# Conditioning matmuls of the second layer: from the first MLP to the stretches between projections, loaded through ScalarE's DMA queue

## The chip, the cores and the metric

The kernel runs on one core of a Trainium2 chip. TensorE (PE in the profile) multiplies; PEld is its loading of weights. VectorE (DVE) and ScalarE (ACT) do the elementwise work, GpSimd (POOL) masks and a few loads, SyncE (SP) issues most loads. The metric is the device time of one execution in microseconds, lower is better.

## What is computed

A decoder step of two layers over 512 prompt tokens and 32 sample tokens (8 sequences of 4), 544 columns in all, in float32. Every sub-layer is wrapped in two RMS norms, and shift, scale and gate come from a conditioning vector per sequence:

```python
def ada_params(c, w, b):
    mod = jax.nn.silu(c) @ w + b
    return jnp.split(mod[:, None, :], 6, axis=-1)
...
for layer in range(DEPTH):
    sh_m, sc_m, g_m, sh_f, sc_f, g_f = ada_params(c, ada_w[layer], ada_b[layer])
    hin = rmsnorm(x, norm_g[layer, 0]) * (1.0 + sc_m) + sh_m
    ...                                   # layer 0: RG-LRU mixer, layer 1: chunked spatial gate
    x = x + g_m * rmsnorm(mix, norm_g[layer, 1])
    hf = rmsnorm(x, norm_g[layer, 2]) * (1.0 + sc_f) + sh_f
    f = jnp.square(jax.nn.relu(hf @ mlp_w_up[layer])) @ mlp_w_down[layer]
    x = x + g_f * rmsnorm(f, norm_g[layer, 3])
```

The weights ada_w of a layer are 1024 x 6144, 25 MB; there are nine conditioning vectors. The six sections of 1024 columns are called sections 0 to 5 below.

## The kernel before

**Projections.** The activations lie transposed: features on partitions, 544 columns in two halves of 272. A large product is split in three (high x high, high x low, low x high), each a matmul of 128 x 128 weights over 272 columns; all go through the helper `mm` (line 119). Weights come through SyncE's queue into wpool (16 buffers), are split by ScalarE (hi, line 181) and VectorE (lo, line 182) ahead of use.

**Clock and tasks.** `mm` also advances a clock by one tick. Side work is written as generators that are added to this clock: each runs a piece, then yields the number of ticks after which its next piece is due. The code's order sets the priority of instructions; the framework that builds the program orders each engine's instructions by that and by when it expects them to be ready, and puts in the waits. Buffers of a pool (gpool has 26, wpool 16, aux two of PSUM, acc three) are given out as they come free.

**Between two projections.** The last projection of a sub-layer (`final_proj`) computes half 0 of all eight row tiles and then half 1 (144 matmuls). For each half a `Chain` follows as a task: root mean square of the result (`Stat`, whose matmul over partitions is line 390), its reciprocal root (lines 412 to 415), the gated residual (lines 660, 662), a second norm, and then, two row tiles at a time, the scaled (line 448) and shifted input HH and HL (lines 452, 453) of the next projection. The next projection begins with `first_sweeps` (288 matmuls): for each half, over four row tiles of weights and then two, first all products with HH, row tile by row tile as the chain brings them, then those with HL. This happens at three places: from the RG-LRU to the first MLP (`final_proj` with (l, idx) = (0, 1)), from the first MLP to the spatial gate (0, 3), and from the spatial gate to the second MLP (1, 1).

**Conditioning.** `ada_gen(jobs, every)` computes blocks of 2048 columns. Per row tile k (eight to a block) it loads 128 x 2048 weights as two tiles of wpool through SyncE's queue (line 598), one step ahead, and issues four matmuls of 128 x 32 by 128 x 512 into four column groups of one aux buffer (line 609). At the end of a block the sums are copied by ScalarE (line 616), transposed (line 620), added with the bias into MOD (`ada_add`, line 568) and derived (`ada_derive`). For layer 1 three such blocks run in the first MLP, a step every 85 ticks, beside `state_out`, which transposes the recurrent states (line 1237) and stores them:

```python
    chains = mlp(0, (1, 0), chains, [ada_gen([(1, 0), (1, 1), (1, 2)], 85), state_out()])
```

`mlp` adds these tasks after its `first_sweeps`.

Of the kernel before, what the change touches and what calls it, by code (L numbers as in the profile page):

```python
# [12 lines left out]
ALU = mybir.AluOpType  # L13
PSUM = bass.MemoryType.PSUM

P = 128
D = 1024
KD = D // P
# [62 lines left out]
def trunk_kernel(  # L81
# [6 lines left out]
    nc = tc.nc  # L88
    V = nc.vector
    A = nc.scalar  # L90
# [13 lines left out]
    def slot(name, dt=F32):  # L104
        return gpool.tile([P, SLOT], dt, tag="s", name=nm(name))
# [4 lines left out]
    def aux():  # L110
        return auxp.tile([P, 512], F32, tag="aux", name=nm("aux"))
# [4 lines left out]
    clk = Clock()  # L116
# [449 lines left out]
    def ada_add(l, sec, kk, nq, src):  # L566
        b = G1[:, kk:kk + nq, 8 + 6 * l + sec:9 + 6 * l + sec]
        V.tensor_tensor(MOD[l][:, sec, kk:kk + nq, :], src, b.to_broadcast([P, nq, 9]), op=ALU.add)

    def ada_derive(l, idx, k0=0, k1=KD):  # L570
        g = G1[:, k0:k1, 4 * l + idx:4 * l + idx + 1].to_broadcast([P, k1 - k0, 9])
        am = AM[l][idx][:, k0:k1]
        V.scalar_tensor_tensor(am, am, 1.0 if idx % 2 == 0 else 0.0, g, op0=ALU.add, op1=ALU.mult)
        V.tensor_scalar(am, am, -0.5, None, op0=ALU.mult)
# [18 lines left out]
    def ada_gen(jobs, every):  # L593
# [10 lines left out]
        for i, (l, blk, k) in enumerate(steps):  # L604
# [21 lines left out]
                ada_derive(l, idx)  # L626
            yield every - 12

    class Chain:


# [55 lines left out]
    def first_sweeps(key, chains, evac):  # L687

        for h in range(2):
            for grp in ((0, 1, 2, 3), (4, 5)):  # L690
                lhs = [st.get(key(m // 2)).lhs(m % 2) for m in grp]
                ps = [acc() for _ in range(len(grp) // 2)]
                for k in range(KD):
                    chains[h].need(k)
                    for i in range(len(grp)):
                        for a in (0, 1):
                            mm(ps[i // 2][:, i % 2, 0:HW], lhs[i][k][a], HH[:, k, HS[h]], k + a == 0, False)
                for i, m in enumerate(grp):
                    for k in range(KD):
                        mm(ps[i // 2][:, i % 2, 0:HW], lhs[i][k][0], HL[:, k, HS[h]], False, k == KD - 1)  # L700
                    if i % 2:
                        for j in range(2):
                            evac(m - 1 + j, ps[i // 2][:, j, 0:HW], h)

    def mix_add(m, ps, first):
# [3 lines left out]
        else:  # L709
            V.tensor_tensor(mv, mv, ps[:, :, 0:HW], op=ALU.add)  # L710

    def final_proj(lhs, rhs, both, groups, l, idx, nxt):


        A.activation(warm, epsc, AF.Abs_reciprocal_sqrt)
        S = [Stat(), Stat(nxt is None)]
        rows = LastRows(AM[l][idx]) if nxt is None else None
        for m in both:
            ps = acc()
            mm3(ps, lhs(m), rhs, (0, 1))  # L720
            mix_add(m, ps, False)
            for h in range(2):
                S[h].add(MIX[:, m, HS[h]])
        if rows:
            rows.add(both)
        chains = []
        for h in range(2):
            for grp, parts in groups[h]:
                if rows and h == 1 and grp[-1] == KD - 1:
                    rows.residual()  # L730
                if rows and h == 1 and grp[-1] == KD - 1:
                    for j, m in enumerate(grp):
                        ps = acc()
                        mm3(ps, lhs(m), rhs, (1,), col=0)
                        V.tensor_tensor(MIX[:, m, HS[1]], MIX[:, m, HS[1]], ps[:, 0, 0:HW], op=ALU.add)
                        S[1].add(MIX[:, m, HS[1]])
                        rows.finish_tile(j)
                    break
                ps = [acc() for _ in range(len(grp) // 2)]
                for ks in parts:  # L740
                    for i, m in enumerate(grp):
                        mm3(ps[i // 2], lhs(m), rhs, (h,), ks=ks, col=i % 2)
                        if i % 2 and ks is parts[-1]:
                            mv = MIX[:, m - 1:m + 1, HS[h]]
                            V.tensor_tensor(mv, mv, ps[i // 2][:, :, 0:HW], op=ALU.add)
                            S[h].add2(mv, slot("sq")[:, 0:T].rearrange("p (j n) -> p j n", j=2))
                            if rows and h == 1:
                                rows.add((m - 1, m))
            if rows and h == 1:
                rows.finish(S[1])  # L750
            else:
                chains.append(Chain(l, idx, S[h], h, nxt))
        return chains
# [497 lines left out]
    def mlp(l, nxt, chains, tasks):  # L1251
        for q in range(4):
            hh, hl = [None] * 8, [None] * 8

            def evac(m, ps, h=None):
                if hh[m] is None:
                    hl[m] = slot("hl", F32R)
                    hh[m] = slot("hh", F32R)
                w = slot("hf")
                if h is None:  # L1260
                    dl, dh, dw = [t_[:, 0:T].rearrange("p (h n) -> p h n", h=2) for t_ in (hl[m], hh[m], w)]
                else:
                    dl, dh, dw = hl[m][:, HS[h]], hh[m][:, HS[h]], w[:, HS[h]]
                A.activation(dw, ps, AF.Relu)  # L1264
                A.activation(dw, dw, AF.Square)
                A.copy(dh, dw)  # L1266
                V.tensor_tensor(dl, dw, f32(dh), op=ALU.subtract)  # L1267

            if q == 0:
                first_sweeps(lambda c: ("u", l, 0, c), chains, evac)  # L1270
                for t in tasks:
                    clk.add(t)
            for c in range(3 if q == 0 else 0, 4):
                u = st.get(("u", l, q, c))
                for j in range(2):
                    ps = acc()
                    mm3(ps, u.lhs(j), hin_rhs, (0, 1))
                    evac(2 * c + j, ps[:, :, 0:HW])
            rhs = list(zip(hh, hl))
            if q == 3:  # L1280
                return final_proj(lambda m: st.get(("d", l, 3, m // 2)).lhs(m % 2), rhs, (0, 1),
                                  (singles(range(2, 8), 8),) * 2, l, 3, nxt)
            for c in range(4):
                u = st.get(("d", l, q, c))
                for j in range(2):
                    ps = acc()
                    mm3(ps, u.lhs(j), rhs, (0, 1))
                    mix_add(2 * c + j, ps, q == 0)
# [79 lines left out]
    def spatial_gate(chains):  # L1368
# [40 lines left out]
            V.bn_stats(stat[0:NSMP, 4, c, :], v)  # L1409

        first_sweeps(lambda c: ("su", c), chains, u_evac)
        t_prep = clk.add(sg_prepare(), 10)
        vts = []
        for c in range(6):
# [139 lines left out]
                nc.sync.dma_start(y_prompt[0, c0:c1, b * 512:(b + 1) * 512], o[0:n, 0:512])  # L1554
                yield 6

    chains = mlp(0, (1, 0), chains, [ada_gen([(1, 0), (1, 1), (1, 2)], 85), state_out()])
    chains = spatial_gate(chains)
    chains = mlp(1, None, chains, [])
    clk.drain(*[t for t in clk.tasks])  # L1560
# [30 lines left out]
```

## Time and profile before

| | |
|---|---|
| median of 3 runs | 1434.71 us (1432.13 to 1434.84) |
| the profiled execution | 1435.27 us, span 1433.5 us |
| TensorE busy | 1395.7 us, 97% of the span |
| VectorE, ScalarE busy | 703.7 us (49%), 632.5 us (44%) |
| moved | 165.71 MB, mean 116 GB/s |

The profile is of one execution. Times in rows are microseconds from the span's start unless they say ns. Busy TensorE is not TensorE at its best, since matmuls overlap and their ends are modelled; the time of a stretch is better read from its length and its count of matmuls. A float32 matmul stands in the rows as two (x8 for four). A row of windows gives the stretch, its length, then busy time (and count of instructions) of PE, PEld, DVE, ACT and POOL, or of those of them that are asked for, then the granted clock of TensorE as a share of 2.4 GHz, the share of the DMA engines and GB/s. An idle time in brackets is that of the engine just before the instruction, with what ended it.

### The profile page before, as it was taken

How to read it: one execution, taken by the hardware profiler on the slowest of the kernel's cores; microseconds unless marked ns; L12 is line 12 of the kernel's file. 1: busy time of each engine (PE TensorE's matmuls, PEld its weight loads, DVE VectorE, ACT ScalarE, POOL GpSimd, SP SyncE). 2: the span in 40 equal slices, each digit the busy share in tenths (PEclk: the TensorE clock that was granted, in tenths of full speed). 3: DMA queues.
4: the chain of work that ended last, by engine and by line, in shares of the span. 5: the costliest groups of instructions: out<-in, count | busy, mean ns of one | idle time of the engine just before them, and what ended most of it. 6: DMA issues, size and time to landing. Idle time of an engine off the chain costs nothing.

```text
span 1433.5 us, 27033 instructions
## 1 busy us (share of the span) xinstructions
PE 1395.7 (97%) x11472; PEld 1319.4 (92%) x11472; DVE 703.7 (49%) x1442; ACT 632.5 (44%) x1160; POOL 41.1 (3%) x76
## 2 busy tenths in 40 slices
PE   8999999998999999999998999999899999999997
PEld 6899989997999999999997989999899999999996
DVE  4767476779422332333349446653972233333334
ACT  4465746846523413414425434432573341432523
POOL 1200000000100000000000200000000000000000
PEclk8999999999999999999999999999999999999998
DMA  9554554321545545543221333122232222222201
GB/s 309 174 173 130 163 151 149 103 89 60 180 154 174 170 157 173 170 157 115 62 86 60 95 96 107 61 74 62 90 100 91 89 89 89 89 89 89 89 1 63
DMA packets 132227, 165.71 MB, mean 116 GB/s; under 512 B 10168, under 2 KB 111560, under 8 KB 132106
## 3 DMA queue, kind: packets, MB, share of 16 engines
q1 hardware_dynamic: 130346, 161.89, 35.9%
q0 software_dynamic: 1760, 2.09, 0.7%
q8 instruction: 90, 1.47, 0.4%
q14 instruction: 31, 0.25, 0.1%
HBM read 161.31 MB, written 2.65 MB: 114 GB/s over the span
## 4 chain that ended last, share of the span: by engine, by line
PE 65%; issue 26%; DVE 5%; ACT 2%; DMA 1%; POOL 0%; SPq 0%; POOLq 0%; ACTq 0%; DVEq 0%
PE acc L119 58%; PE aux L609 3%; DVE lo L182 1%; PE acc L1478 1%; DVE MIX L448 1%; DVE X L662 1%; DMA xsr<-in_x_sample_dram 1%; DVE HL L453 1%; PE aux L1397 0%; PE aux L580 0%; DVE MIX L660 0%; PE aux L390 0%; ACT HH L452 0%; DVE rs L414 0%; DVE R L415 0%
## 5 line engine op out<-in xcount | busy, mean ns | idle before, releaser
L119 PE MATMUL acc<-HH,hi 128*128 128x272 f32 x1776 | 399.2, 293 | 12.6 <-ACT HH L452 11.2
L119 PE MATMUL acc<-HH,lo 128*128 128x272 f32 x1776 | 394.0, 292 | 3.4 <-DVE lo L182 3.4
L182 DVE TENSOR_TENSOR lo<-raw,hi 128x512 fp32r<-128x512 f32 (+1 forms) x404 | 263.2, 682 | 254.3 <-ACT hi L181 188.1
L119 PE MATMUL acc<-HL,hi 128*128 128x272 f32 x1776 | 355.4, 289 | 3.5 <-DVE HL L453 3.1
L181 ACT CAST hi<-raw 128x512 fp32r<-128x512 f32 (+1 forms) x404 | 230.3, 613 | 281.7 <-PE acc L119 159.2
L119 PEld LDWEIGHTS acc<-HH,hi 128*128 128x128 f32 x1776 | 293.6, 191 | 23.2 <-ACT HH L452 13.7
L119 PEld LDWEIGHTS acc<-HH,lo 128*128 128x128 f32 x1776 | 293.1, 191 | 11.5 <-issue 6.7
L119 PEld LDWEIGHTS acc<-HL,hi 128*128 128x128 f32 x1776 | 273.5, 189 | 10.9 <-issue 5.4
L119 PE MATMUL acc<-hh,lo 128*128 128x272 f32 x1024 | 230.0, 290 | 0.0
L119 PE MATMUL acc<-hh,hi 128*128 128x272 f32 x1024 | 229.8, 290 | 0.0
L119 PE MATMUL acc<-hl,hi 128*128 128x272 f32 x1024 | 229.7, 290 | 0.0
L119 PEld LDWEIGHTS acc<-hh,hi 128*128 128x128 f32 x1024 | 168.0, 188 | 3.9 <-issue 3.8
L119 PEld LDWEIGHTS acc<-hh,lo 128*128 128x128 f32 x1024 | 168.1, 188 | 3.7 <-issue 3.6
L119 PEld LDWEIGHTS acc<-hl,hi 128*128 128x128 f32 x1024 | 168.1, 188 | 3.6 <-issue 3.5
L1267 DVE TENSOR_TENSOR hl<-hf,hh 128x544 fp32r<-128x544 f32 (+1 forms) x76 | 47.7, 634 | 175.2 <-ACT hh L1266 175.0
L1264 ACT ACTIVATE hf<-acc 128x544 f32<-128x544 f32 (+1 forms) x76 | 41.2, 550 | 128.1 <-PE acc L119 126.1
L710 DVE TENSOR_TENSOR MIX<-MIX,acc 128x544 f32<-128x544 f32 x44 | 31.6, 717 | 75.9 <-PE acc L119 75.9
L119 PE MATMUL acc<-hi,HH 128*128 128x256 f32 x192 | 54.8, 285 | 0.0
L119 PE MATMUL acc<-hi,HL 128*128 128x256 f32 x192 | 54.6, 284 | 0.0
L119 PE MATMUL acc<-lo,HH 128*128 128x256 f32 x192 | 53.8, 280 | 0.0
L119 PE MATMUL acc<-yh,hi 128*128 128x272 f32 x208 | 52.7, 291 | 0.3 <-ACT MIX L708 0.3
L119 PE MATMUL acc<-yh,lo 128*128 128x272 f32 x208 | 52.6, 291 | 0.0
(332 smaller groups left out, 1444.5 us busy)
## 6 DMA issues: line engine op xcount, KB each, us to landing
ada<-in_ada_w_dram SPq DMA_DIRECT2D x96, 512.0 KB, 4.9
raw<-in_mlp_w_up_dram SPq DMA_DIRECT2D x64, 512.0 KB, 4.3
raw<-in_mlp_w_down_dram SPq DMA_DIRECT2D x64, 512.0 KB, 4.5
raw<-in_lru_w_in_dram SPq DMA_DIRECT2D x24, 512.0 KB, 4.5
raw<-in_sg_w_in_dram SPq DMA_DIRECT2D x24, 512.0 KB, 4.6
raw<-in_sg_w_out_dram SPq DMA_DIRECT2D x12, 512.0 KB, 4.2
raw<-in_lru_w_out_dram SPq DMA_DIRECT2D x8, 384.0 KB, 3.0
raw<-in_lru_w_out_dram SPq DMA_DIRECT2D x6, 512.0 KB, 6.4
```

The lines of the kernel that those rows point to most:

```text
L119: nc.tensor.matmul(out, lhsT, rhs, start=start, stop=stop)
L181: A.copy(h_, raw[:, c:c + st])
L182: V.tensor_tensor(l_, raw[:, c:c + st], f32(h_), op=ALU.subtract)
L448: V.scalar_tensor_tensor(wv, X[:, k, c0:c1], Am[:, k, 0:1], R[:, c0:c1], op0=ALU.mult, op1=ALU.mult)
L453: V.scalar_tensor_tensor(HL[:, k, c0:c1], wv, sh[:, k, 0:1], f32(HH[:, k, c0:c1]), op0=ALU.add, op1=ALU.subtract)
L609: nc.tensor.matmul(ps[32 * g:32 * g + 32, :], scT[:, k, :], ts_[g // 2][:, (g % 2) * 512:(g % 2) * 512 + 512], start=(k == 0), stop=(k == ...
L662: V.scalar_tensor_tensor(X[:, j, c0:c1], MIX[:, j, c0:c1], Gm[:, j, 0:1], X[:, j, c0:c1], op0=ALU.mult, op1=ALU.add)
L710: V.tensor_tensor(mv, mv, ps[:, :, 0:HW], op=ALU.add)
L1264: A.activation(dw, ps, AF.Relu)
L1267: V.tensor_tensor(dl, dw, f32(dh), op=ALU.subtract)
L1478: nc.tensor.matmul(ps[p0:p0 + 32, 0, ck * P:(ck + 1) * P], vp[ck // 2, c][:, o:o + 32], wT[g], start=True, stop=True, tile_position=(0, p0))
```

## The change

A new generator `ada_fill(l, c0, n)` computes n columns of a layer's conditioning from column c0. It takes a step of four matmuls of the same shape as ada_gen's, of which four times 256 KB of weights are loaded into four slots of gpool ("adf") through ScalarE's DMA queue, one step ahead; 52 ticks lie between steps. With n = 2048 the four column groups of the aux buffer are four blocks of 512 columns, eight steps in all; with n = 1024 they are two blocks of columns for two row tiles at once, four steps, and two of the groups are added by VectorE at the end. The buffer is held from the first step to the last.

Three fills for layer 1 start with the second half of a final projection: sections 0 and 1 at (0, 1), sections 2 and 3 at (0, 3), section 5 at (1, 1). Each is drained behind the first_sweeps that follow. Section 4 is a task of the first MLP, in the place of the three blocks of ada_gen. Layer 0's conditioning stays as it was.

```diff
--- before.py
+++ after.py
@@ -625,6 +625,41 @@
             for idx in ((0,), (1,), (2, 3))[blk]:
                 ada_derive(l, idx)
             yield every - 12
+
+    def ada_fill(l, c0, n, wait=52):
+
+
+        kk = 4096 // n // 2
+        nb = n // 512
+        for k0 in range(0, KD, kk):
+            ts_ = [slot("adf") for _ in range(4)]
+            for g in range(4):
+                k, c = k0 + g // nb, c0 + (g % nb) * 512
+                nc.scalar.dma_start(ts_[g][:, 0:512], ada_w[l, k * P:(k + 1) * P, c:c + 512])
+            yield wait
+            if k0 == 0:
+                ps = aux()
+            for g in range(4):
+                nc.tensor.matmul(ps[32 * g:32 * g + 32, :], scT[:, k0 + g // nb, :], ts_[g][:, 0:512],
+                                 start=(k0 == 0), stop=(k0 + kk == KD), tile_position=(0, 32 * g))
+        raw = slot("adas")
+        A.copy(raw[:, 0:512], ps)
+        yield 12
+        pt = aux()
+        for q in range(4):
+            nc.tensor.transpose(pt[:, q * P:(q + 1) * P], raw[:, q * P:(q + 1) * P], ident)
+        ptv = pt.rearrange("p (q g s) -> p q g s", q=4, g=4)
+        for g in range(4):
+            c = c0 + (g % nb) * 512
+            sec, kt = c // D, (c % D) // P
+            if g < nb:
+                ada_add(l, sec, kt, 4, ptv[:, :, g, 0:9])
+            else:
+                m_ = MOD[l][:, sec, kt:kt + 4, :]
+                V.tensor_tensor(m_, m_, ptv[:, :, g, 0:9], op=ALU.add)
+        for sec in range(c0 // D, (c0 + n) // D):
+            if sec in (1, 2, 4, 5):
+                ada_derive(l, (1, 2, 4, 5).index(sec))
 
     class Chain:
 
@@ -709,6 +744,9 @@
         else:
             V.tensor_tensor(mv, mv, ps[:, :, 0:HW], op=ALU.add)
 
+    fills = {}
+    FILL = {(0, 1): (1, 0, 2048), (0, 3): (1, 2048, 2048), (1, 1): (1, 5 * D, 1024)}
+
     def final_proj(lhs, rhs, both, groups, l, idx, nxt):
 
 
@@ -725,6 +763,8 @@
             rows.add(both)
         chains = []
         for h in range(2):
+            if h == 1 and (l, idx) in FILL:
+                fills[l, idx] = clk.add(ada_fill(*FILL[l, idx]))
             for grp, parts in groups[h]:
                 if rows and h == 1 and grp[-1] == KD - 1:
                     rows.residual()
@@ -1268,6 +1308,7 @@
 
             if q == 0:
                 first_sweeps(lambda c: ("u", l, 0, c), chains, evac)
+                clk.drain(fills[l, 1])
                 for t in tasks:
                     clk.add(t)
             for c in range(3 if q == 0 else 0, 4):
@@ -1409,6 +1450,7 @@
             V.bn_stats(stat[0:NSMP, 4, c, :], v)
 
         first_sweeps(lambda c: ("su", c), chains, u_evac)
+        clk.drain(fills[0, 3])
         t_prep = clk.add(sg_prepare(), 10)
         vts = []
         for c in range(6):
@@ -1554,7 +1596,7 @@
                 nc.sync.dma_start(y_prompt[0, c0:c1, b * 512:(b + 1) * 512], o[0:n, 0:512])
                 yield 6
 
-    chains = mlp(0, (1, 0), chains, [ada_gen([(1, 0), (1, 1), (1, 2)], 85), state_out()])
+    chains = mlp(0, (1, 0), chains, [ada_fill(1, 4 * D, 1024), state_out()])
     chains = spatial_gate(chains)
     chains = mlp(1, None, chains, [])
     clk.drain(*[t for t in clk.tasks])
```

## Rows read from the trace of the kernel before

**Rows 1.** page, busy time of each engine; the chain that ended last, by engine
```profile
PE 1395.7 (97%) x11472; PEld 1319.4 (92%) x11472; DVE 703.7 (49%) x1442; ACT 632.5 (44%) x1160; POOL 41.1 (3%) x76
...
PE 65%; issue 26%; DVE 5%; ACT 2%; DMA 1%; POOL 0%; SPq 0%; POOLq 0%; ACTq 0%; DVEq 0%
```

**Rows 2.** windows, line 119 alone, over equal parts of the two MLPs
```profile
378.91:711.82 332.91, 309.36 (x2403) 302.72 (x2401) 1.00 0.47 151
1068.13:1369.38 301.25, 301.25 (x2403) 301.25 (x2402) 1.00 0.28 86
```

**Rows 3.** the same window of the first MLP, lines 609, 620, 1237
```profile
378.91:711.82 332.91, 25.58 (x192) 3.79 (x192) 1.00 0.47 151
...
378.91:711.82 332.91, 1.80 (x12) 1.42 (x12) 1.00 0.47 151
...
378.91:711.82 332.91, 2.39 (x16) 1.62 (x16) 1.00 0.47 151
```

**Rows 4.** chain of waits, two pieces: start us, us, what
```profile
397.48 0.99 PE aux L609 x8
398.47 10.96 PE acc L119 x85
```

**Rows 5.** windows, all engines, the three stretches between projections
```profile
324.00:358.00 34.00, 27.40 (x187) 25.82 (x186) 32.21 (x76) 20.23 (x46) 0.00 (x0) 0.90 0.20 63
755.00:783.00 28.00, 22.44 (x165) 20.17 (x164) 26.39 (x61) 15.19 (x32) 0.00 (x0) 1.00 0.25 77
1012.00:1046.00 34.00, 26.04 (x172) 24.46 (x172) 32.38 (x76) 20.37 (x46) 1.02 (x2) 0.91 0.21 66
```

**Rows 6.** timeline of TensorE, 327 to 356 us: start, duration, [idle before]
```profile
327.66 0.59 PE L119 MATMUL acc<-HH,hi 128*128 128x272 f32 x1 [3.02 <-ACT HH L452]
...
351.95 1.03 PE L1237 MATMUL aux<-ident,HST 128*9 128x128 f32 x8
...
353.90 0.39 PE L119 MATMUL acc<-HH,hi 128*128 128x272 f32 x1 [0.92 <-ACT HH L452]
...
355.88 0.39 PE L119 MATMUL acc<-HH,hi 128*128 128x272 f32 x1 [0.71 <-ACT HH L452]
```

**Rows 7.** windows, VectorE alone, before the last holes of A and C
```profile
312.00:348.00 36.00, 35.78 (x77) 0.91 0.23 74
...
1001.00:1037.00 36.00, 35.93 (x77) 0.95 0.25 77
```

**Rows 8.** waits of SyncE's queue: us in total, times, longest
```profile
SPq L598 <- PE acc L119: 99.2, 21, 14.3
...
SPq L598 <- PE aux L609: 82.8, 13, 11.5
```

**Rows 9.** line 568: duration ns min/median/max, first and last start
```profile
L568 DVE TENSOR_TENSOR MOD<-aux,G x24: 180/184/196, 16.4 to 663.1; 128x36 f32<-128x36 f32 x24
```

**Rows 10.** DMA issues of lines 598 and 1554, ns min/median/max, and landing
```profile
L598 SPq DMA_DIRECT2D ada<-in_ada_w_dram x44: 327/341/1056, 385.3 to 639.9; - x44
...
DMA to landing us min/median/max: 3.8/4.7/6.6
...
L1554 SPq DMA_DIRECT2D out_dram<-yo x6: 325/334/366, 1404.1 to 1411.6; - x6
```

**Rows 11.** timeline of ScalarE in A: start, duration, [idle before]
```profile
311.32 0.66 ACT L365 ACTIVATE sq<-MIX 128x544 f32<-128x544 f32 x1 [1.81 <-DVE MIX L745]
...
327.09 1.35 ACT L452 ACTIVATE HH<-MIX,MOD 128x272 fp32r<-128x272 f32 x3 [0.96 <-DVE MIX L448]
...
329.56 0.52 ACT L452 ACTIVATE HH<-MIX,MOD 128x272 fp32r<-128x272 f32 x1 [1.13 <-DVE MIX L448]
```

**Rows 12.** windows, all engines, stretches of half clock (PEclk)
```profile
328.00:333.00 5.00, 5.00 (x23) 5.00 (x23) 5.00 (x11) 2.64 (x6) 0.00 (x0) 0.50 0.24 59
1016.00:1019.00 3.00, 3.00 (x15) 3.00 (x15) 3.00 (x8) 1.57 (x4) 0.00 (x0) 0.51 0.00 0
1043.40:1046.40 3.00, 2.67 (x12) 2.67 (x13) 3.00 (x9) 2.97 (x9) 0.00 (x0) 0.50 0.00 0
```

## The prediction

> **What bounds the kernel now.** I read the page first: TensorE is busy for 97% of the span, and the chain that ended last runs over it [rows 1]. So time can only come out of TensorE's queue, either as work taken away or as idle time filled. Next I read windows over the two MLPs, which are the same code. Over equal counts of projection matmuls (2403 each) the first MLP takes 332.91 us and the second 301.25 us [rows 2]; the second has no idle time at all and runs at 301.25 / 2403 = 0.125 us a matmul. The 31.66 us between them are what ada_gen and state_out put into the first: 24 steps of four conditioning matmuls on line 609, three groups of transposes on line 620 and four on line 1237 [rows 3]. The chain of waits shows how such a step sits in the dense stream: 0.99 us of line 609, then 85 projection matmuls in 10.96 us [rows 4]. Third, windows over the three places where one projection ends and the next begins. There, and only there, TensorE idles: 34.00 - 27.40 = 6.6 us around 324 to 358, 5.6 us around 755 to 783, 8.0 us around 1012 to 1046 [rows 5]. I call them A, B and C. The timeline of A shows the idle time as separate holes, ended by ScalarE's HH [rows 6]. VectorE is the reason: in the 36 us up to the last hole it is busy for 35.8 us and more [rows 7]. These stretches are set by VectorE and ScalarE, the MLPs by TensorE.
>
> **What leaves the first MLP.** A group of transposes takes 1.80 / 3 = 0.60 us, one of state_out 2.39 / 4 = 0.60 us [rows 3]. The rest of the difference gives the price of a step, its switches to and fro included: (31.66 - 7 x 0.60) / 24 = 1.14 us. The new fill for section 4 keeps four steps and one group of transposes in the first MLP. So 20 steps and two groups leave: 20 x 1.14 + 2 x 0.60 = 24.0 us, all from a stretch where TensorE never idles. SyncE also loses 48 loads of 512 KB, and the buffers of wpool they took; the waits for those buffers are long [rows 8], but they stood behind a full TensorE, so I count nothing for them.
>
> **What enters A, B and C.** The fills of A and B have eight steps and one group, that of C four and one: 2 x (8 x 1.14 + 0.60) + 4 x 1.14 + 0.60 = 24.6 us. With nothing hidden the change is worth +0.6 us. What counts is where the steps fall. A fill starts with the second half of a final projection, 144 matmuls before the sweeps, which are 288. With wait=52 its matmuls come due at 53, 105, 157, 209, 261, 313, 365 and 417: two in the projection's second half, then at 13, 65, 117, 169, 221 and 273 of the sweeps. The last hole of A, at 355.88 [rows 6], is at the third of eight row tiles of the second half's sweep, about 160. So five steps stand before the last hole, three steps and the transposes behind it.
>
> The order on an engine is not that of the code: the transposes of state_out are added after the first sweeps, and yet they run at 351.95 in A, ahead of the sweep's second half [rows 6]. Ready work is thus put into holes, and I expect the norms' own matmuls to keep their place, as soon as VectorE has their sums, although two steps now stand before them. Then five steps, 5.7 us, fit into the holes of A (6.6 us) and nearly into those of B (5.6 us), and C's four steps and transposes, 5.2 us, fit into 8.0 us. The three late steps and the transposes are exposed in A and B: 2 x (3 x 1.14 + 0.60) = 8.0 us.
>
> What those holes already hold has to move: 1.03 us of state_out's transposes in A [rows 6], and I take as much for the sample columns' matmuls (line 1397) in B. These take an aux buffer, of which there are two, and a fill holds one from its first step to its last. I count 2.0 us for them; 0 is the lower bound, if they still find a hole.
>
> A fill's last step costs VectorE four additions of 0.18 us [rows 9] and as many small derivations, and ScalarE one copy; there are four fills where there were three blocks. They stand at the end of the sweeps, or in the MLP, where neither engine is late. Nothing.
>
> **The loads on ScalarE's queue.** No row shows a load issued by ScalarE. SyncE spends 0.34 us on one (0.33 us for the 256 KB stores of line 1554) [rows 10]. Four to a step are 1.34 us in which ScalarE starts nothing else, and behind them on its queue stand the squares, the reciprocal roots and the HH activations that VectorE and then TensorE wait for. Bounds: 0, if all fall into its idle time, and 20 x 1.34 = 26.8 us, if every load delays the chain. In between the rows decide: before the squares of the second half it idles 1.81 us, before HH 0.96 and 1.13 us [rows 11]. The first two loads of a fill go into the long gaps and cost nothing. The next three (two in C), eight in all, stand ahead of HH and cost 1.34 less some 0.88 us of idle time: 8 x 0.46 = 3.7 us. One more in A and in B meets a busy ScalarE behind the evacuations, 0.5 us each. I take 4.7 us, near the lower bound, because those gaps are what the loads are nearest to.
>
> The weights must also land in time. Loads of 512 KB land 4.7 us after issue in the first MLP, at most 6.6 us [rows 10]; a step comes 52 x 0.125 = 6.5 us and more after its loads. No wait, if the loads are issued on time. The Trainium skill, page "DMA: Bandwidth & Descriptors", section "Issuing engines are not separate DMA queues", says that loads from several engines share the same 16 DMA engines, and that another issuing engine saves only issue time. By it the new queue brings no bandwidth, which the sum above does not count either; no row of this kernel has loads from ScalarE to test it.
>
> **Sum.** -24.0 + 8.0 + 2.0 + 4.7 = -9.3 us. The profiled execution took 1435.27 us (span 1433.5), so 1426.0 us; the median of the runs is 1434.71, 0.6 us lower, which I leave inside the range.
>
> **Rivals.** *ScalarE becomes the bound (slower).* Its loads may have to wait for a buffer, and everything behind them waits too. In the kernel before, 34 of the 80 loads of ada_gen waited on SyncE for TensorE to free a buffer, 182 us in total [rows 8], which cost nothing there. The same on ScalarE would stop the chain of norms. The new tiles come from gpool, 26 slots, of which 16 hold hh and hl in B until the projection ends: ten are left, four to a step. Against it: in A only six slots hold yh and yl. From 14.0 / 20 = 0.70 us of exposed time a step the gain is gone; at 1.34 us a step the time is 1435.27 - 24.0 + 8.0 + 2.0 + 26.8 = 1448.1 us. The page "TensorE: Matmul & The Clock Gate" of the Trainium skill, section "Architectural detail: the array is 16x 32x32, not 1x 128x128", calls ScalarE's queue strictly first in, first out, which speaks for this rival: a load that waits would hold up all behind it. No row here has a load on that queue to show it. Chance 0.18.
>
> *The work only changes places (same).* If steps delay the norms' own matmuls, VectorE starts later by as much, and the holes stay: 24.6 - 24.0 = +0.6, 1435.9 us. For it: TensorE reaches each norm's matmul just as its sums are ready. Against it: the displaced transposes above. Chance 0.16.
>
> *More is hidden (faster still).* If late steps are pulled forward as state_out's transposes were, only what exceeds the holes remains: A 9.7 - 7.6, B 9.7 - 6.6 (with the space of the displaced work), 5.2 us in all, and 2.0 us for that work: 1435.27 - 24.0 + 7.2 = 1418.5 us, with ScalarE's loads free. TensorE also runs at a granted clock of 0.5 (its 1.2 GHz level) after holes in A and twice in C [rows 12]; 12 matmuls and more in the last of these, at about 0.22 (5.0 / 23 in A) instead of 0.125 us, are worth another 1 to 1.7 us if the clock stays up. The earlier two are followed by waits for VectorE anyway. About 1417 us. Chance 0.13.
>
> **Numbers.** The forecast has 0.53 and its own range is 1419 to 1432 us. A kernel can be told from no change from about 0.2%, 2.9 us. Faster: 0.53 + 0.13 = 0.66; same 0.16; slower 0.18. The range reaches to the rival below it, and above to the first part of ScalarE's: 1415 to 1438 us, which leaves out its dearer half and a little at the low end.
>
> **What would show it.** In the first MLP: no line 609 of the second layer, and the 2403 matmuls of [rows 2] in 309 to 311 us. Idle TensorE in A, B and C together down from 20.1 us to 7 or less, with A and B each 4 to 7 us longer and C about equal. ScalarE rows with "DMA" issues ahead of HH, and idle time of VectorE ended by ScalarE where there was none. If TensorE shows gaps ended by a landing of adf, or ScalarE's issues wait for line 119, the ScalarE rival is at work; if A and B grow by 10 us each with unchanged holes, the work only moved.

## The result and the profile after

The changed kernel takes 1447.23 us, the median of 4 runs (1445.75 to 1451.49), against 1434.18 us for the kernel before. The ratio is 1.0096, with a 95% interval of 1.0084 to 1.0108: a little slower, by 1%, where the forecast was 1426.0 us and faster. The profiled execution took 1446.72 us (span 1445.0).

The page of the changed kernel, its lines on the busy time, the chain by engine, and the group of the moved matmuls, to be held against [rows 1, 3]:

```profile
PE 1420.8 (98%) x11476; PEld 1316.8 (91%) x11476; DVE 705.2 (49%) x1446; ACT 631.6 (44%) x1161; POOL 41.5 (3%) x76
...
PE 70%; issue 26%; ACT 1%; DVE 1%; DMA 1%; POOL 0%; SPq 0%; POOLq 0%; ACTq 0%; DVEq 0%
...
L643 PE MATMUL aux<-adf,scT 128*32 128x512 f32 x192 | 57.5, 605 | 0.0
```

TensorE is busy for 1420.8 us where it was 1395.7, with all but the same instructions. The third line says where: the 192 records of the second layer's 24 steps (four matmuls each, a float32 matmul counts as two records; 20 of the steps were moved, four stay in the MLP) keep TensorE busy for 57.5 us. In the kernel before the same 192 records took 25.58 us [rows 3]. One record lasts 605 ns here, and 605 ns in the kernel before, where the group of both layers' steps is

```profile
L609 PE MATMUL aux<-ada,scT 128*32 128x512 f32 x320 | 43.5, 605 | 0.0
```

What has changed is how many of them run at the same time.

The first MLP did what was forecast. Windows over line 119 alone, between the same matmuls as in [rows 2]:

```profile
392.59:701.14 308.55, 303.54 (x2402) 301.67 (x2401) 1.00 0.31 97
```

332.91 - 308.55 = 24.4 us left it; the prediction took 24.0. Nearly all else is in the three stretches. Here are windows between the same projection matmuls of the two kernels, from A's first sweep to the start of the MLP's window, and from ahead of the steps of B and C to where they are over; first before, then after. The columns are the window, its length, the busy time of TensorE, of its weight loads, VectorE, ScalarE and GpSimd, the granted clock, and DMA:

```profile
327.66:378.91 51.25, 47.66 (x348) 46.30 (x349) 40.28 (x91) 30.50 (x73) 2.01 (x4) 0.94 0.38 120
740.14:831.17 91.03, 85.47 (x670) 79.56 (x668) 65.60 (x155) 46.34 (x91) 9.81 (x16) 1.00 0.27 81
1000.20:1060.04 59.84, 51.88 (x373) 50.17 (x372) 54.52 (x120) 37.74 (x84) 2.50 (x5) 0.94 0.27 81
sum 202.12, PE 185.01 PEld 176.04 DVE 160.40 ACT 114.58 POOL 14.31; mean PE 61.67 PEld 58.68 DVE 53.47 ACT 38.19 POOL 4.77
```

```profile
328.81:392.59 63.78, 62.41 (x396) 46.75 (x397) 41.12 (x98) 33.53 (x80) 1.95 (x4) 1.00 0.51 166
729.46:837.29 107.83, 107.83 (x739) 83.10 (x737) 67.25 (x161) 46.96 (x92) 10.14 (x16) 1.00 0.45 140
1006.31:1071.54 65.23, 60.63 (x409) 50.38 (x408) 55.39 (x125) 37.69 (x85) 2.53 (x5) 0.97 0.38 124
sum 236.84, PE 230.88 PEld 180.23 DVE 163.76 ACT 118.17 POOL 14.63; mean PE 76.96 PEld 60.08 DVE 54.59 ACT 39.39 POOL 4.88
```

A, B and C grew by 12.5, 16.8 and 5.4 us, 34.7 us in all. The first steps of A's fill stand ahead of A's window, in the second half of the projection; over its 144 matmuls, first before, then after (the window, its length, busy time of TensorE, clock, DMA):

```profile
305.17:327.67 22.50, 19.48 (x151) 0.97 0.15 47
302.52:328.82 26.30, 25.50 (x171) 1.00 0.50 161
```

That is 3.8 us more, and 38.5 us in all, where the prediction has 8.0 + 2.0 + 4.7 = 14.7. The holes are filled: idle time in the three windows falls from 202.12 - 185.01 = 17.1 to 6.0 us, and the clock of A and C is mostly back (1.00 and 0.97 for 0.94). And yet it is slower, 38.5 - 24.4 = +14.1 us. The spans show 1445.0 - 1433.5 = 11.5 of it, since the profiled execution of the changed kernel is 2.6 us ahead after the first 400 projection matmuls (91.22 us for 93.84), before anything that the change moved. TensorE is busy for 45.9 us more in the three windows.

Why, the timeline of TensorE in A shows (start, duration, operation, count; rows of line 119 left out between):

```profile
336.62 0.29 PE L119 MATMUL acc<-HH,lo 128*128 128x272 f32 x1
336.75 0.65 PE L390 MATMUL aux<-pt,dmean 128*128 128x272 f32 x2
337.32 1.04 PE L643 MATMUL aux<-adf,scT 128*32 128x512 f32 x2
338.30 0.40 PE L119 MATMUL acc<-HH,hi 128*128 128x272 f32 x1
...
339.50 1.05 PE L643 MATMUL aux<-adf,scT 128*32 128x512 f32 x4
340.49 0.39 PE L119 MATMUL acc<-HH,hi 128*128 128x272 f32 x1
340.72 0.28 PE L119 MATMUL acc<-HH,lo 128*128 128x272 f32 x1
340.93 1.04 PE L643 MATMUL aux<-adf,scT 128*32 128x512 f32 x2
341.91 0.39 PE L119 MATMUL acc<-HH,hi 128*128 128x272 f32 x1
```

One step, of four matmuls in four column groups of 32, stands there in three pieces, x2, x4 and x2, with projection matmuls between. Each piece takes 1.04 to 1.05 us, as long as the x8 of a whole step, 1.06 us in the same trace (0.99 us of it stand in the chain of [rows 4]). Next to each other the four share the time; apart, each piece pays it whole. In the order of TensorE's program the 24 steps stand in 54 such pieces, and 57.5 / 54 = 1.06 us: 15 steps of A, B and C lie in three pieces each, and nine steps are whole, among them the four in the MLP. The Trainium skill says this in "TensorE: Matmul & The Clock Gate", section "Part 3: Packing small matmuls — row/col tiling": matmuls at different tile positions run at the same time, a pack lasts about as long as one of them, and matmuls start and end in program order. The trace agrees (1.06 us for x8, 1.04 us for x2), and shows what follows when another matmul comes between.

ScalarE changed too. Its timeline at the start of A (ACTq are the loads that it issues):

```profile
316.96 0.93 ACTq L638 DMA_DIRECT2D adf<-in_ada_w_dram  x2
322.04 0.49 ACT L412 ACTIVATE R<-aux,epsc 128x272 f32<-128x272 f32 x1 [5.28 <-PE aux L390]
322.43 0.61 ACT L181 CAST hi<-raw 128x512 fp32r<-128x512 f32 x1
322.57 0.34 ACTq L638 DMA_DIRECT2D adf<-in_ada_w_dram  x1
```

For 5.28 us, part of them spent on issuing loads, it starts no work of its own until the reciprocal root of a norm (L412), and the splits of the next weights (L181) stand behind that root. In the kernel before, four of these splits come ahead of it:

```profile
319.31 1.12 ACT L181 CAST hi<-raw 128x512 fp32r<-128x512 f32 x2
321.96 1.14 ACT L181 CAST hi<-raw 128x512 fp32r<-128x512 f32 x2 [1.53 <-issue]
323.05 0.49 ACT L412 ACTIVATE R<-aux,epsc 128x272 f32<-128x272 f32 x1
```

So there are two theories. **T**: the steps fall apart, and their pieces cost. **S**: the loads cost on ScalarE's queue, for the splits and HH behind them. The prediction has a term for this, 4.7 us, and its first rival has more.

### The profile page after: what moved, and what is told of

Its sections match the earlier page's. It is cut to its first block, busy times and chain, and to the rows that moved or that the text cites. A ratio compares the mean times of both kernels' runs of the same rounds, so it can differ in the third digit from the quotient of the medians.

```text
span 1445.0 us, 27085 instructions
## 1 busy us (share of the span) xinstructions
PE 1420.8 (98%) x11476; PEld 1316.8 (91%) x11476; DVE 705.2 (49%) x1446; ACT 631.6 (44%) x1161; POOL 41.5 (3%) x76
## 4 chain that ended last, share of the span: by engine, by line
PE 70%; issue 26%; ACT 1%; DVE 1%; DMA 1%; POOL 0%; SPq 0%; POOLq 0%; ACTq 0%; DVEq 0%
PE acc L119 61%; PE aux L643 4%; PE aux L609 1%; PE acc L1520 1%; PE aux L580 1%; DMA xsr<-in_x_sample_dram 1%; PE aux L390 0%; PE aux L1438 0%; PE aux L531 0%; DVE lo L182 0%; PE aux L1444 0%; PE aux L1402 0%; PE aux L966 0%; PE aux L1277 0%; DVE MIX L448 0%
## 5 line engine op out<-in xcount | busy, mean ns | idle before, releaser
L119 PE MATMUL acc<-HH,hi 128*128 128x272 f32 x1776 | 394.8, 291 | 5.5 <-ACT HH L452 4.0
L181 ACT CAST hi<-raw 128x512 fp32r<-128x512 f32 (+1 forms) x404 | 230.7, 613 | 281.5 <-PE acc L119 223.8
L119 PEld LDWEIGHTS acc<-HH,hi 128*128 128x128 f32 x1776 | 289.9, 189 | 27.6 <-ACT HH L452 10.7
L119 PEld LDWEIGHTS acc<-HH,lo 128*128 128x128 f32 x1776 | 289.7, 189 | 17.4 <-issue 12.6
L643 PE MATMUL aux<-adf,scT 128*32 128x512 f32 x192 | 57.5, 605 | 0.0
```

Source lines behind the costliest of these rows:

```text
L119: nc.tensor.matmul(out, lhsT, rhs, start=start, stop=stop)
L181: A.copy(h_, raw[:, c:c + st])
L643: nc.tensor.matmul(ps[32 * g:32 * g + 32, :], scT[:, k0 + g // nb, :], ts_[g][:, 0:512], start=(k0 == 0), stop=(k0 + kk == KD), tile_posit ...
```

## The experiments

A ratio is always to the kernel before on the same chip.

**Steps together, ScalarE's queue.**

```diff
-            for g in range(4):
-                nc.tensor.matmul(ps[32 * g:32 * g + 32, :], scT[:, k0 + g // nb, :], ts_[g][:, 0:512],
-                                 start=(k0 == 0), stop=(k0 + kk == KD), tile_position=(0, 32 * g))
+            for g in (3, 2, 1, 0):
+                m4 = nc.tensor.matmul(ps[32 * g:32 * g + 32, :], scT[:, k0 + g // nb, :], ts_[g][:, 0:512],
+                                      start=(k0 == 0), stop=(k0 + kk == KD), tile_position=(0, 32 * g))
+                if g < 3:
+                    tc.keep_in_program_order(m4)
```

> The changed kernel, with the four matmuls of every moved step kept next to each other in TensorE's program (issued in the order 3, 2, 1, 0, each pinned behind the one before), loads and queue as they are. Theory T (the steps fall apart): the trace of the changed kernel shows the 24 moved steps in 54 pieces, and a piece of one, two or four matmuls costs about 1.07 us alike. Here they stand in 24 pieces, so TensorE has 30 x 1.07 = 32 us less to do; up to 13 us of holes that the loose pieces had filled and some 4 us of clock may come back. That gives 1447 - 32 + 0 to 17 = 1415 to 1432 us. Rival S (ScalarE's queue: the 96 load issues hold back ScalarE's splits, and so the projections): the issues are the same, so 1447 within 3 us.

Measured: 1433.54 us, 1.0000 of before (0.9985 to 1.0015). Its group of the moved matmuls, and the sum of the windows over the same three stretches:

```profile
L643 PE MATMUL aux<-adf,scT 128*32 128x512 f32 x192 | 27.0, 637 | 9.6 <-DMA adf<-in_ada_w_dram 9.3
```

```profile
sum 222.51, PE 205.02 PEld 177.90 DVE 165.61 ACT 118.05 POOL 14.57; mean PE 68.34 PEld 59.30 DVE 55.20 ACT 39.35 POOL 4.86
```

The 57.5 us become 27.0, and 13.7 us of time come back, so T holds. The result is just above T's upper end, 1432 us: of the 30.5 us, more than expected is lost to idle time, which is 222.51 - 205.02 = 17.5 us, as much as before the change. TensorE now waits 9.3 us for loads of adf, which is no part of T.

**The same in the kernel before.** Eight steps in the first MLP, with six projection matmuls between the four of a step:

```diff
+            split = (l, blk) == (1, 1)
             for g in range(4):
-                nc.tensor.matmul(
+                m4 = nc.tensor.matmul(
...
+                if split:
+                    tc.keep_in_program_order(m4)
+                    if g < 3:
+                        yield 6
...
-                yield every
+                yield every - (18 if split else 0)
```

> The kernel before, its middle block of conditioning (eight steps in the first MLP) with the four matmuls of each step emitted six projection matmuls apart, loads and all else as before: 24 more pieces. Theory T: 24 x 1.05 = 25 us more, 1435 + 25 = 1460 us (1455 to 1463), and the page shows 32 single pieces of about 1.07 us. Rival S and the prediction's pricing (a step costs 1.14 us for four matmuls wherever they stand, so 0.27 each): 1435 within 3 us.

Measured: 1463.91 us, 1.0210 of before (1.0194 to 1.0226), 0.9 us above T's range. Two pieces of the timeline, the group of all 320 records, which was 43.5 us before, and TensorE over the same projection matmuls of the first MLP, before and here:

```profile
511.35 1.04 PE L610 MATMUL aux<-ada,scT 128*32 128x512 f32 x2
513.27 1.04 PE L610 MATMUL aux<-ada,scT 128*32 128x512 f32 x2
```

```profile
L610 PE MATMUL aux<-ada,scT 128*32 128x512 f32 x320 | 68.4, 604 | 0.0
```

```profile
378.91:712.20 333.29, 333.29 (x2626) 1.00 0.47 150
378.67:739.88 361.21, 361.21 (x2626) 1.00 0.44 139
```

24 more pieces add 24.9 us to the group, 1.04 each, and 27.9 us to the MLP, 1.16 each: the switches to and from the projection come on top. This is the full price where nothing is idle, and as much as the prediction's 1.14 us for a whole step. (The time grew by 30.3 us; 1.2 us of it lie in C, where nothing was changed, and the rest is within the spread of the runs.) T is shown, with no load on ScalarE's queue at all.

**Steps together, SyncE's queue.**

```diff
-                nc.scalar.dma_start(ts_[g][:, 0:512], ada_w[l, k * P:(k + 1) * P, c:c + 512])
+                nc.sync.dma_start(ts_[g][:, 0:512], ada_w[l, k * P:(k + 1) * P, c:c + 512])
...
```

> The changed kernel with the four matmuls of each step kept together, and with the 96 loads issued by SyncE's DMA queue in place of ScalarE's. Theory T: as the run with ScalarE's queue, within 3 us, since what costs is TensorE's pieces. Rival S: faster than that run by what the issues cost on ScalarE: 4.7 us by the prediction's term, up to 26.8 us by its upper bound. A third way: SyncE's queue is in order, so that a load that waits for its buffer holds up the weights behind it; then slower, by an amount no row gives.

Measured: 1420.77 us, 0.9911 of before (0.9890 to 0.9932). This is 12.8 us less than from ScalarE's queue, so S holds as well, and T alone is not enough. The same two views as above:

```profile
L643 PE MATMUL aux<-adf,scT 128*32 128x512 f32 x192 | 25.6, 605 | 1.9 <-DMA adf<-in_ada_w_dram 1.9
```

```profile
sum 211.10, PE 200.88 PEld 175.22 DVE 164.39 ACT 117.67 POOL 14.22; mean PE 66.96 PEld 58.41 DVE 54.80 ACT 39.22 POOL 4.74
```

Idle time is 10.2 us instead of 17.5, the waits for adf are 1.9 us instead of 9.3, and the clock is 1.00 in all three windows instead of 0.97 to 0.98. The three stretches grew by 211.10 - 202.12 = 9.0 us (A 5.7, B 4.0, C -0.7); the prediction without its term for ScalarE has 10.0 (5.0, 5.0 and 0).

**Steps apart, SyncE's queue.** The same edit in the changed kernel alone.

> The changed kernel with the 96 loads on SyncE's queue, and the matmuls of a step free to fall apart (42 pieces in this program's order, where the changed kernel has 54 and the run with steps kept together 24). If the two costs found so far add up (13.7 us for 30 pieces, so 0.46 each after what holes give back, and 12.8 us for ScalarE's queue): 1447.2 - 12.8 - 12 x 0.46 = 1429 us (1427 to 1434). If the pieces cost only because loads on ScalarE's queue came late: 1421 within 2 us, as with steps together on SyncE's queue.

Measured: 1435.47 us, 1.0013 of before (1.0003 to 1.0022). That is 1.5 us above the expected range and 6.5 us above its centre, so a piece costs more here than the 0.46 us it was put at: 14.7 / 18 = 0.82 us, by the square below. The square reads:

| | ScalarE's queue | SyncE's queue |
|---|---|---|
| steps apart | 1447.2 | 1435.5 |
| steps together | 1433.5 | 1420.8 |

Apart costs 13.7 and 14.7 us, ScalarE's queue 11.8 and 12.8 us more than SyncE's. The two nearly add, but not because they have nothing to do with each other. With the steps apart, the group of line 643 is 46.0 us here against 57.5: SyncE's queue gains 11.5 us by fewer pieces (42 for 54), and its idle time in the three windows is no smaller (7.0 us for 6.0). With the steps together it gains by fewer holes (10.2 us for 17.5). Loose pieces had filled the holes that ScalarE's lateness made.

**Loads alone.** The kernel before, with the 80 loads of A, B and C beside it and nothing that needs them, from ScalarE's queue (as written here), then from SyncE's, then from ScalarE's with 16 columns for 512, 8 KB each:

```diff
...
+        for k0 in range(0, KD, kk):
+            ts_ = [slot("adf") for _ in range(4)]
+            for g in range(4):
+                k, c = k0 + g // nb, c0 + (g % nb) * 512
+                nc.scalar.dma_start(ts_[g][:, 0:512], ada_w[l, k * P:(k + 1) * P, c:c + 512])
+            yield wait
+            for g in range(4):
+                nc.gpsimd.tensor_copy(sink, ts_[g][:, 0:1])
...
```

> The kernel before, its second layer's matmuls and their loads in the first MLP as they were, and beside them the changed kernel's 80 loads of stretches A, B and C from ScalarE's queue, whose data nothing uses (GpSimd reads one column of each). It leaves the output as it is. If ScalarE's queue costs by what it keeps from its other work (12.8 us between the two runs with steps together, of which about 6 us are TensorE's own waits for these loads, which cannot occur here): 1434 + 5 to 8 = 1439 to 1442 us. If only the lateness of the loads costs: 1434 within 2 us.

> The same 80 unused loads beside the kernel before, from SyncE's queue: if it is the queue's engine that costs, 1434 within 2 us; if it is the traffic (20 MB more) or the buffers that they hold, as much as the run from ScalarE's queue.

> The run with 80 unused loads from ScalarE's queue beside the kernel before (1446.5 us), each cut from 512 columns to 16 (8 KB instead of 256 KB). It leaves the output as it is. If the 12.7 us come from the issues standing on ScalarE's queue: 1446 within 3 us. If they come from transfers that have to land, or from traffic: 1434 to 1437 us.

Measured: 1446.51 us from ScalarE (1.0083 of before, 1.0066 to 1.0100), 1436.72 us from SyncE (1.0013, 1.0003 to 1.0022), 1438.72 us for the small ones (1.0029, 1.0018 to 1.0041). Beside their own runs of before that is 12.7, 2.9 and 4.1 us. The first is more than the 5 to 8 us expected, the second is just above its 2 us, and the third lies between its two cases. So the loads cost 12.7 us with no matmul behind them, and 9.8 us of it go with ScalarE's queue rather than SyncE's, where the changed kernel showed 11.8 to 12.8. The 2.9 us are traffic, the buffers held and GpSimd's reads of the loads. (The splits take their slots from gpool too; but SyncE's loads hold as many, and A is as long with them as before, 51.25 us for 51.24.) The issues are 4.1 us at most, since the small loads hold buffers and are read too, and have moved two splits, as the second timeline below shows. What remains goes with the size of the loads, though the issues do not: their median is 390 ns in both. ScalarE's timeline with 256 KB, then with 8 KB:

```profile
319.58 1.78 ACTq L640 DMA_DIRECT2D adf<-in_ada_w_dram  x4
324.77 0.49 ACT L412 ACTIVATE R<-aux,epsc 128x272 f32<-128x272 f32 x1 [4.54 <-PE aux L390]
325.16 0.61 ACT L181 CAST hi<-raw 128x512 fp32r<-128x512 f32 x1
```

```profile
317.99 1.78 ACTq L640 DMA_DIRECT2D adf<-in_ada_w_dram  x4
319.87 1.15 ACT L181 CAST hi<-raw 128x512 fp32r<-128x512 f32 x2 [1.23 <-DMA adf<-in_ada_w_dram]
322.30 0.49 ACT L412 ACTIVATE R<-aux,epsc 128x272 f32<-128x272 f32 x1 [1.28 <-PE aux L390]
```

With the small loads two splits still stand ahead of the root, with the large ones the next splits all stand behind it, as in the changed kernel; with SyncE's loads four stand ahead of it, as before. What the order alone costs can be tried without any load.

**Splits behind the root.** The kernel before, each split pinned behind the last root in the code:

```diff
-                    A.copy(h_, raw[:, c:c + st])
+                    cp = A.copy(h_, raw[:, c:c + st])
+                    if last_r:
+                        tc.add_manual_dep(cp.ins, last_r[-1].name, mybir.DependencyInfo(
+                            mybir.DependencyClass.NoSync, mybir.DependencyReason.DATA), reason="behind_r")
...
-        A.activation(out, ms, AF.Abs_reciprocal_sqrt, bias=epsc)
+        last_r.append(A.activation(out, ms, AF.Abs_reciprocal_sqrt, bias=epsc).ins)
```

> The kernel before with nothing moved, but each split of a weight tile (ScalarE's copy to hi) pinned behind the reciprocal root of a norm that the code has ahead of it. In the kernel before ScalarE does such splits while it would wait for that norm's matmul; in the changed kernel and in the run with 256 KB unused loads they stand behind it, in the run with 8 KB loads (4.1 us) ahead of it. If this order is what the larger loads cost beyond their issues: 1434.6 + 8 = 1442 us (1439 to 1446), and VectorE's lo and TensorE behind it wait in A. If the order costs nothing, and the landing does: 1434.6 within 2 us.

Measured: 1440.52 us, 1.0046 of before (1.0031 to 1.0060), so +6.5 us for order alone, within the range expected. Waits of TensorE from 318 to 362 us in this run:

```profile
PE acc L120 <- ACT HH L456: 3.8, 3, 2.6
PE acc L120 <- DVE lo L186: 2.1, 3, 1.0
PE acc L120 <- DVE HL L457: 1.0, 1, 1.0
PE acc L120 <- ACT hi L182: 0.6, 1, 0.6
```

TensorE now waits three times for lo, 2.1 us, where it waited once for 1.0 us before, and once for the split itself. With up to 4.1 us for the issues and up to 2.9 us for traffic and buffers, which these 4.1 in part contain, this comes to 13.5 us at most, and to less by what the parts share, against 12.7. That is a sum of separate runs, not shown in one. By stretch it comes out only roughly: with 256 KB from ScalarE A, B and C are 5.0, 2.7 and 1.9 us longer than before, from SyncE 0.0, -0.5 and 1.5, with small loads 1.6, 1.8 and -1.1, with the pinned splits 2.4, 2.3 and 1.6. The pin moves the splits further than the loads did in places, so 6.5 us is the price of about this order, not of exactly that one.

**Half the issues.** Steps together, ScalarE's queue, two loads of 512 KB for a step:

```diff
-            ts_ = [slot("adf") for _ in range(4)]
-            for g in range(4):
-                k, c = k0 + g // nb, c0 + (g % nb) * 512
-                nc.scalar.dma_start(ts_[g][:, 0:512], ada_w[l, k * P:(k + 1) * P, c:c + 512])
+            ts_ = []
+            for i in range(2):
+                t2 = wtile("adf")
+                k, c = k0 + 2 * i // nb, c0 + (2 * i % nb) * 512
+                nc.scalar.dma_start(t2, ada_w[l, k * P:(k + 1) * P, c:c + 1024])
+                ts_ += [t2[:, 0:512], t2[:, 512:1024]]
...
```

> Steps together, loads on ScalarE's queue as in the changed kernel, but two of 512 KB for a step in place of four of 256 KB, into the tiles that the weights use (48 issues for 96). ScalarE's queue has cost 12.8 us with 96 issues. If it costs by the issue: 1420.8 + 6.4 = 1427 us. If an issue's time goes with the bytes: 1433 as before. If the issues wait for the weights' buffers, as SyncE's did in the kernel before: above 1434.

Measured: 1433.97 us (0.9995, 0.9986 to 1.0005), as with four loads, but not because an issue's time goes with the bytes: an issue of 512 KB took 334 ns in the median, one of 256 KB 442 ns, so the time of issuing fell from 96 x 0.44 = 42 us to 16 us and nothing came back. TensorE still waits 8.7 us for adf. This does not tell why, for something else came in: these tiles are the weights', and ScalarE's queue stands still in front of 16 of the 48 issues, 24.0 us in all, each time until TensorE or VectorE lets it go on, by the times of their semaphores (with four loads 0.3 us in all). At the start of A four splits stand ahead of the root here, as in the kernel before, and it is no faster.

**ScalarE's queue in the MLP.** The kernel before with the conditioning loads of the second layer issued by ScalarE:

```diff
-                nc.sync.dma_start(ts_[i], ada_w[l, k * P:(k + 1) * P, c:c + 1024])
+                (nc.scalar if l == 1 else nc.sync).dma_start(ts_[i], ada_w[l, k * P:(k + 1) * P, c:c + 1024])
```

> The kernel before with the 48 loads of 512 KB of the second layer's conditioning issued by ScalarE's queue, matmuls in the first MLP as they were. If an issue costs where ScalarE is behind only (A, B, C), and TensorE has work in the MLP: 1434.6 within 2 us. If ScalarE stands still while a load waits for its buffer (the prediction's first rival; on SyncE these waits were 182 us): slower, 1440 us or more.

Measured: 1434.97 us, 1.0005 of before (0.9996 to 1.0014). ScalarE's queue stood still ahead of 20 of the 48 issues, 24.4 us in all, until TensorE or VectorE let it go on. Where TensorE has work for a long time ahead, 48 loads on ScalarE's queue cost nothing, these waits included.

**A's steps back in the MLP.** From the best run so far (steps together, SyncE's queue), the eight steps of A go back (chain_of runs one generator after the other):

```diff
...
-    FILL = {(0, 1): (1, 0, 2048), (0, 3): (1, 2048, 2048), (1, 1): (1, 5 * D, 1024)}
+    FILL = {(0, 3): (1, 2048, 2048), (1, 1): (1, 5 * D, 1024)}
...
-    chains = mlp(0, (1, 0), chains, [ada_fill(1, 4 * D, 1024), state_out()])
+    chains = mlp(0, (1, 0), chains, [chain_of(ada_gen([(1, 0)], 85), ada_fill(1, 4 * D, 1024)), state_out()])
```

> The run with steps kept together and loads on SyncE's queue, but the eight steps of stretch A done in the first MLP as in the kernel before; B, C and the four steps of the MLP stay. In the trace of that run A has cost 9.3 us, as much as eight steps and transposes cost in the MLP (8 x 1.14 + 0.60 = 9.7). If A hides nothing: 1420.8 + 0.4 = 1421 within 2 us. If A hides five of its eight steps, as the prediction took it: 1420.8 + 5 x 1.14 = 1426.5 us.

Measured: 1425.29 us (0.9942, 0.9927 to 0.9958). So A is worth 4.5 us (4.4 by the spans of the two profiles), nearer to the five hidden steps of the prediction, 5.7 us, than to none. That is about four of eight steps, with a wide margin: the intervals of the two ratios, 0.9890 to 0.9932 and 0.9927 to 0.9958, touch. (The 9.3 us of the expectation were read over windows that reach into the MLP; between the same matmuls A grew by 5.7 us.)

**Earlier loads, and a third queue.** Steps together, loads issued one step ahead from SyncE's queue; and without that, from GpSimd's queue:

```diff
...
+        nxt = load(0)
+        for k0 in range(0, KD, kk):
+            ts_, nxt = nxt, load(k0 + kk) if k0 + kk < KD else None
...
```

> Steps together and loads on SyncE's queue, each step's loads issued one step earlier (two steps' tiles held instead of one). In the run without this TensorE still waits 1.9 us in stretch A for loads of adf. If the steps then also fall into holes: 1420.8 - 1.9 = 1419 us (1417 to 1421). If eight instead of four of the 26 slots hold up the projection's own tiles: slower than 1420.8.

> Steps together, the 96 loads issued by GpSimd's queue (GpSimd is busy 3% of the span). If what costs on ScalarE is only that its own work stands behind the issues: as on SyncE's queue, 1421 within 2 us. If a load from GpSimd's queue is dearer or lands later than SyncE's: slower, TensorE's waits for adf show by how much.

Measured: 1420.33 us (0.9898, 0.9883 to 0.9913) and 1418.92 us (0.9888, 0.9874 to 0.9903). Loading earlier takes TensorE's waits for adf away (0.0 us) and gains 0.4 us, less than the runs can tell. GpSimd's queue does at least as well as SyncE's, with no wait for adf either:

```profile
L643 PE MATMUL aux<-adf,scT 128*32 128x512 f32 x192 | 25.6, 605 | 0.0
```

This version beats both kernels, the one before by 15.7 us in its own comparison, the changed one by 28.3 us (two comparisons).

## Why the prediction was wrong

*What leaves the first MLP* was right: 24.4 us for 24.0, and 308.55 us in [rows 2]'s window, just below the 309 to 311 us named.

*What enters A, B and C* is the step that failed: 38.5 us came in, where the sum has 14.7. It priced each of 20 steps at 1.14 us, a price read in the MLP [rows 3, 4], where the four matmuls of a step stand next to each other. The sum has no term for a step that comes apart, though the change gives each matmul a load of its own, where two matmuls shared one. That the framework takes each matmul when it expects its load is argued from this, and a load of its own is not enough: nine steps have four loads too and are whole, four of them in the MLP, where TensorE is never idle. The 54 pieces and their price are shown. The step's own observation, that ready work is put into holes, should have raised the question whether a piece of a step may be put there too. The pieces cost 31.9 us of TensorE's time and, since they filled holes, 13.7 to 14.7 us of the kernel's.

*Five steps hidden in A*, with the steps kept whole: 4.5 us against 5.7, nearly right. *Idle time down to 7 us or less* came true (6.0 us in the windows above), and for the wrong reason: loose pieces fit into holes better than steps, and a step in three pieces costs three times as much. Filled holes were no sign of a gain. (The prediction says that TensorE idles only in A, B and C. Of its 37.8 us of idle time 5.9 lie ahead of the first projection matmul and 10.3 behind the last; the change touches neither.)

*The loads on ScalarE's queue* is the second term that failed: the bounds, 0 to 26.8 us, hold, but 4.7 us were taken and 11.8 to 12.8 us measured. The issues, which are all that the term counts, cost 4.1 us at most in the run with small loads; that this is near 4.7 may be luck, since the 0.88 us of idle time in that sum stand in no row ([rows 11] has 0.96 and 1.13, which would make it 3.4 us), and an issue took 0.44 us for its 0.34. Missed were the splits of the weights, which the new loads put behind the roots on ScalarE's queue, 6.5 us when done alone.

Without its 4.7 us for ScalarE the sum gives 1421.3 us; steps together on SyncE's queue measured 1420.8, and its three stretches come out within 1.1 us each. So the rest of the working holds, and the 26.5 us between that run and the changed kernel are the two costs above, about half each. The page that the prediction cites, "DMA: Bandwidth & Descriptors" of the Trainium skill, section "Issuing engines are not separate DMA queues", says that another issuing engine brings no DMA engines of its own. The runs agree in that loads from ScalarE's queue gained nothing over SyncE's (1433.5 against 1420.8 us); what they take from their own engine, these runs show.

*The rivals.* ScalarE as the bound was put at 1448.1 us, and the time came out there by luck, not by the mechanism: no issue of the changed kernel took longer than 1.27 us, its queue stood still ahead of issues for 0.6 us in all, and ScalarE's share is under half of 26.8 us. "The work only changes places" (1435.9 us) has the time of the run with steps together on ScalarE's queue, 1433.5 us, and its holes as before; but 9.3 us of TensorE's idle time end with a landing of adf there, not with the norms. "More is hidden" is near in number to the best version, 1418.9 for about 1417 us; its stretches grew by 8.1 us, where that rival has 7.2 less 1 to 1.7 for the clock.

What stays open: why the larger loads move the splits in the framework's order, and how ScalarE's 11.8 to 12.8 us divide. The runs show that the loads move the splits, and the price of about this order, not the choice behind it.

## What to carry to other kernels

Small matmuls in different column groups are cheap only next to each other, so before moving them into a stretch where the order is the framework's, pin them together and count the pieces in the order that comes out. A loss of this kind shows as busy time: look at the busy time of the moved group before and after, not only at the holes. Put added loads on a queue whose engine has nothing behind them that is waited for; here half a microsecond of issuing cost less (4.1 us at most) than the reordering that came with it (6.5 us alone).

## What the runs showed of the hardware

A lone 128x32 by 128x512 float32 matmul keeps TensorE as long as four in four column groups: 1.04 us against 1.06 us in the same trace, and 1.16 us of time with the switches around it. An issue of 256 KB from GpSimd took 536 ns in the median against 442 ns on ScalarE and 385 ns on SyncE (the three runs with steps together), and its loads landed in 4.5 us, against 4.0 and 5.4 us. An issue's time did not grow with the bytes: on ScalarE 390 ns for 8 KB and for 256 KB in the runs with unused loads, 334 ns for 512 KB.
